# A diffusion trunk on eight cores: the context block projected before its shift is known, loads in order of need, output stores without waits

## Chip, cores, metric

One Trainium2 chip, eight cores (two dies of four). Every core runs the same program on its own share. The metric is device time in microseconds (us) of the slowest core. Some executions fall into a slower state, in which the cores of one die show a lower granted clock; those runs are marked slow and left out of every comparison and every median below (among them one execution each of e1, e6, e10 and e12, two of e2, and some of the kernel before). Ratios below are the mean time of one kernel's fast runs over that of the other's fast runs of the same rounds, so not quite the ratio of the medians that are quoted.

## The reference, cut to what matters

Two layers; each is a mixer and a SwiGLU feed-forward, each sub-layer normalised, modulated by conditioning and added through a gate. One core holds 512 context tokens (**block 0**) and 1024 latent tokens (**blocks 1 and 2**), of 1024 channels.

```python
def ada_terms(cond, w, b):          # six (Bc, 1, D) arrays: shift/scale/gate for mixer and ffn
    mod = (jax.nn.silu(cond) @ w + b)[:, None, :]
    return jnp.split(mod, 6, axis=-1)
# mixer of layer 0:  h = rms_norm(x, g) * (1 + scale) + shift
#   z = h @ w_in                    # pooling input, query, key/value latent, rotary key
#   pooling mixer on z[:512]; multi-head latent attention on the rest
#   context attends to itself; latent attends to 512 cached tokens and its own 1024
# layer 1 mixer: chunked spatial-gating MLP (gMLP). After each mixer: SwiGLU feed-forward.
```

The context's compressed keys and rotary keys of layer 0 are outputs too (`state_ckv`, `state_krope`).

## The kernel before

A Python class writes the instruction streams of the engines. Each piece of work is a generator that yields a unit (`U`) when it needs an engine, a buffer or a PSUM bank. A list scheduler picks the next unit by estimated times; among these is a model of how transfers of the two issuing queues share the DMA engines. So **the order of instructions on each engine follows from the model's constants**, and for some copies and squares the engine too. A different estimate gives a different order in all that follows.

```python
    DMA_RATE = 335.0
    def dma(self, q, out, in_, key, after=None):
        ...
        if last is not None and last != nm and self.known[q].get(k, 0) < self.dtot[k]:
            eng.wait_ge(self.sem[k], self.dtot[k])      # same semaphore, other tile: wait for all before
        ...
        self.queues[q].append([self.t[q] + 300.0, n * esize(in_.dtype) / self.DMA_RATE, ev])
    def _flow(self):                                    # the model of two queues that share the engines
        ...
            if on_a and on_b:
                d = min(ra, rb) * 2
                ra -= d / 2
                rb -= d / 2
    ...
        def load_w0():                                  # weights of the first projections
            yield U("dma")
            P.dma("pool", cb[:], cb_d, "cb")
            yield U("dma", cond=lambda: 7 in ada_ring or st["ada"] >= 8)   # after eight conditioning pieces
            W["ina"] = Multi(P, "w_ina", 8, 672, BF16, 3)
            ... # w_ina (3 loads), w_ukv, cached latent, then the cached rope key krr[3], w_uq, rope tables, w_inu, pool_w
        def k_rope(kb):
            yield U("dve", cond=has("kv%d" % kb), room=(1024, 1024))
            kr = krr[kb]
            sqk = P.alloc("sqkr", [32, 512], BF16)
            kg = P.alloc("kg", [32, 512], BF16)
            P.square(sqk[:], kr[:], engs=("dve", "act"))                   # reads the loaded key
    ...
            # last group of the last feed-forward, block b, row tile m
            resid(ps, l, 5, m, b)
            if store and lastg:
                P.dma("sp", y_out[b, m], x[b][:, m, :], "yout")
    ...
            (0, load_x("xi", (0, 1, 2), {1: landed("d_ada5"), 2: landed("d_wina2")})),   # when x of blocks 1, 2 may start
```

Of the kernel before, what the change touches and what calls it, by code (L numbers as in the profile page):

```python
# [22 lines left out]
def esize(dt):  # L23
    return 2 if dt == BF16 else 4
# [54 lines left out]
class Prog:  # L79


    DMA_RATE = 335.0
# [314 lines left out]
    def dma(self, q, out, in_, key, after=None):  # L397
# [10 lines left out]
        if last is not None and last != nm and self.known[q].get(k, 0) < self.dtot[k]:  # L408
            eng.wait_ge(self.sem[k], self.dtot[k])
            self.known[q][k] = self.dtot[k]  # L410
            evs = evs + [(k, self.dtot[k])]
# [10 lines left out]
        self.queues[q].append([self.t[q] + 300.0, n * esize(in_.dtype) / self.DMA_RATE, ev])  # L422
# [10 lines left out]
    def _flow(self):  # L433

        ia, ib = 0, 0
        A, B = self.queues["sp"], self.queues["pool"]
        t, ra, rb = 0.0, (A[0][1] if A else 0.0), (B[0][1] if B else 0.0)
        while ia < len(A) or ib < len(B):
# [4 lines left out]
            if on_a and on_b:  # L443
                d = min(ra, rb) * 2
                ra -= d / 2
                rb -= d / 2
# [180 lines left out]
def build():  # L627
# [32 lines left out]
    with ExitStack() as es:  # L660
# [16 lines left out]
        P.memset("dve", ones[:], 1.0)  # L677
        EPSI = {1024: 0, 384: 1, 256: 2, 96: 3}
# [20 lines left out]
        ada_ring = {}  # L699
        hid = [{}, {}]  # L700
# [5 lines left out]
        def ada_dma():  # L706
            for k in range(48):
                yield U("dma", room=(lambda: [4096] + keep(0)) if k >= 20 else 4096, cond=lambda k=k: k < 8 or (k < st["ada"] + 3 and (k < 20 or "ffn0" in flags) and "win_loaded" in flags))
                ada_ring[k] = P.alloc("adaw", [128, 8, 256], BF16)
                P.dma("pool", ada_ring[k][:], ada_d[k], "ada%d" % (k % 8))  # L710
# [3 lines left out]
        def ada():  # L714
            for k in range(48):
# [4 lines left out]
                l, c0 = divmod(2 * k, 48)  # L720
# [8 lines left out]
                for (l_, w, n) in ((0, 0, 8), (0, 1, 20), (1, 0, 32), (1, 1, 44)):  # L729
# [21 lines left out]
        def xnorm(l, w, b, cond, done, last=False):  # L751
            need = {(0, 0): 8, (0, 1): 20, (1, 0): 32, (1, 1): 44}[(l, w)]
# [29 lines left out]
            for kc in range(8):  # L782
                if last:
                    yield U(("dve", "act"), reads=[xb[:, kc, :]])
                    P.affine(hb[:, kc, :], xb[:, kc, :], AA[:, l, w, kc, ci:ci + 1], mscal(l, sh, kc, b))
# [5 lines left out]
                P.back(tmp)  # L791
            if last:
# [4 lines left out]
            flags.add(done)  # L797

# [13 lines left out]
        def load_w0():  # L812
            yield U("dma")
            P.dma("pool", cb[:], cb_d, "cb")
            yield U("dma", cond=lambda: 7 in ada_ring or st["ada"] >= 8)
# [3 lines left out]
            flags.add("ina_loaded")  # L819
            W["ukv"] = P.alloc("w_ukv", [128, 2, 1024], BF16)  # L820
            P.dma("pool", W["ukv"][:], wukv_d, "wukv")
            ckvn[3] = P.alloc("ckvn", [128, 2, 512], BF16)
            P.dma("pool", ckvn[3][:], cckv, "cckv")
            krr[3] = P.alloc("krr", [32, 512], F32)
            P.dma("sp", krr[3][:], ckr, "ckr")
            flags.add("kv3")
            W["uq"] = P.alloc("w_uq", [128, 3, 768], BF16)
            P.dma("pool", W["uq"][:], wuq_d, "wuq")
# [4 lines left out]
            W["inu"] = Multi(P, "w_inu", 8, 512, BF16, 4)  # L833
            for q in range(2):
                P.dma("pool", W["inu"].tiles[q][:], wiu_d[:, 4 * q:4 * q + 4, :], "winu%d" % q)
            W["pw"] = P.alloc("pw", [128, 4, 128], BF16)
            P.dma("pool", W["pw"][:], pw_d, "pw")
            flags.add("win_loaded")

        rope, ckvn, cqn, krr, uT = {}, {}, {}, {}, {}  # L840

        def win_norm(b, j0, nj, dst, g0, nn, copy=None):
# [3 lines left out]
            for j in range(nj):  # L846
# [4 lines left out]
                ps = pss[j]  # L851
                P.mmg(ps[:], [(wa[:, kc, (j0 + j) * 128:(j0 + j + 1) * 128], hb[:, kc, :]) for kc in range(8)])
                sq = P.tmp(BF16)
                P.square(sq[:], ps[:])
                sqs.append(sq)
# [15 lines left out]
        def win_q(b):  # L871
# [4 lines left out]
            drop("h%d" % b, 3, h[b])  # L876
            drop("ina", 6, W["ina"])

        def win_kv(b):
# [5 lines left out]
            yield U("pe", reads=[hb[:], wa[:]], bank=1)  # L885
            ps = P.bank()
            P.mmg(ps[0:32, :], [(wa[:, kc, 640:672], hb[:, kc, :]) for kc in range(8)])
# [736 lines left out]
```

## Time and profile before

| | before |
|---|---|
| time, fast runs | 1264.77 to 1265.47 us |
| profiled run, span of the slowest core (core 0) | 1268.0 us |
| TensorE busy, share of the span | 90% |
| first projection matmul, median of 8 cores | 68.2 us |
| long attention (blocks 1 and 2), first and last score matmul, median | 192.4 and 350.4 us |
| first matmul of the first feed-forward, median | 389.3 us |
| end of TensorE's last matmul, median | 1245.0 us |

The milestones come from TensorE's instructions on all eight cores. They say where the time lies better than shares do: the head (to 68), the mixer of layer 0 (to 389), the dense rest, and a tail in which only stores run. The lines are shown in the prediction.

### The profile page before, as it was taken

How to read it: one execution, taken by the hardware profiler on the slowest of the kernel's cores; microseconds unless marked ns; L12 is line 12 of the kernel's file. 1: busy time of each engine (PE TensorE's matmuls, PEld its weight loads, DVE VectorE, ACT ScalarE, POOL GpSimd, SP SyncE). 2: the span in 40 equal slices, each digit the busy share in tenths (PEclk: the TensorE clock that was granted, in tenths of full speed). 3: DMA queues.
4: the chain of work that ended last, by engine and by line, in shares of the span. 5: the costliest groups of instructions: out<-in, count | busy, mean ns of one | idle time of the engine just before them, and what ended most of it. 6: DMA issues, size and time to landing. Idle time of an engine off the chain costs nothing.

```text
span 1268.0 us, 15934 instructions; the slowest of 8 cores (1254.1 to 1268.0 us)
## 1 busy us (share of the span) xinstructions
PE 1135.3 (90%) x5849; PEld 509.5 (40%) x5849; DVE 575.4 (45%) x960; ACT 383.3 (30%) x611; POOL 186.4 (15%) x286
## 2 busy tenths in 40 slices
PE   2178976998889999999999998999899999999995
PEld 1033433333234545444444433444444444444442
DVE  0068767645137312241342587675542134134264
ACT  2146665768943111101101063343321110110100
POOL 5334223330020120100100000220401010000000
PEclk9998986999999999999999998999899999999998
DMA  9970263360079999630555010000826062030004
GB/s 176 208 165 26 38 110 70 62 205 1 1 109 169 169 171 165 103 64 1 91 97 104 2 34 1 1 1 1 139 45 116 1 112 38 1 67 1 1 17 183
DMA packets 31001, 97.03 MB, mean 77 GB/s; under 512 B 4288, under 2 KB 5856, under 8 KB 30928
## 3 DMA queue, kind: packets, MB, share of 16 engines
q0 software_dynamic: 21424, 73.58, 34.8%
q1 hardware_dynamic: 9504, 22.44, 5.7%
q8 instruction: 50, 0.82, 0.3%
q14 instruction: 23, 0.19, 0.1%
HBM read 159.19 MB, written 6.88 MB: 131 GB/s over the span
## 4 chain that ended last, share of the span: by engine, by line
PE 75%; DVE 9%; DMA 7%; ACT 4%; issue 2%; POOL 0%; SPq 0%; ACTq 0%; DVEq 0%; POOLq 0%
PE pp L492 75%; DMA adaw_106<-ada_w 2%; DMA krr_131<-ckr 2%; DMA adaw_4159<-ada_w 2%; ACT pt_1380 L511 1%; ACT pt_1379 L511 1%; ACT pt_1381 L511 1%; DMA qT_627<-tb_68 1%; DMA qT_1382<-tb_70 1%; ACT pt_1378 L511 1%; DVE tf_81 L526 0%; DVE tf_82 L526 0%; DVE tf_79 L526 0%; DVE tf_77 L526 0%; SPq L413 0%
## 5 line engine op out<-in xcount | busy, mean ns | idle before, releaser
L511 ACT ACTIVATE tf_79<-pp 128x512 f32<-128x512 f32 x22 | 13.1, 597 | 185.4 <-PE pp L492 185.4
L511 ACT ACTIVATE tf_80<-pp 128x512 f32<-128x512 f32 x23 | 13.7, 597 | 65.7 <-PE pp L492 65.7
L511 ACT ACTIVATE tf_77<-pp 128x512 f32<-128x512 f32 x23 | 13.7, 597 | 65.2 <-PE pp L492 65.1
L511 ACT ACTIVATE tf_82<-pp 128x512 f32<-128x512 f32 x22 | 13.1, 597 | 62.7 <-PE pp L492 62.7
L511 ACT ACTIVATE tf_78<-pp 128x512 f32<-128x512 f32 x22 | 13.1, 597 | 62.5 <-PE pp L492 62.5
L511 ACT ACTIVATE tf_81<-pp 128x512 f32<-128x512 f32 x20 | 11.9, 597 | 60.4 <-PE pp L492 60.4
L515 DVE TENSOR_TENSOR sqkr_160<-krr_131 32x512 bf16<-32x512 f32 x1 | 0.7, 678 | 54.3 <-DMA krr_131<-ckr 54.3
L526 DVE SCALAR_TENSOR_TENSOR x_2288<-pp,mod_47,x_2288 128x512 f32<-128x512 f32 x20 | 15.0, 751 | 14.3 <-PE pp L492 13.8
L526 DVE SCALAR_TENSOR_TENSOR x_2285<-pp,mod_47,x_2285 128x512 f32<-128x512 f32 x20 | 15.0, 751 | 14.3 <-PE pp L492 13.8
L526 DVE SCALAR_TENSOR_TENSOR x_2286<-pp,mod_47,x_2286 128x512 f32<-128x512 f32 x20 | 15.0, 751 | 14.2 <-PE pp L492 13.7
L526 DVE SCALAR_TENSOR_TENSOR x_2287<-pp,mod_47,x_2287 128x512 f32<-128x512 f32 x20 | 15.0, 750 | 13.7 <-PE pp L492 13.3
L526 DVE SCALAR_TENSOR_TENSOR x_2413<-pp,mod_47,x_2413 128x512 f32<-128x512 f32 x20 | 15.0, 750 | 12.3 <-PE pp L492 12.0
L526 DVE SCALAR_TENSOR_TENSOR x_2429<-pp,mod_47,x_2429 128x512 f32<-128x512 f32 x20 | 14.9, 751 | 11.6 <-PE pp L492 11.3
L526 DVE SCALAR_TENSOR_TENSOR x_2414<-pp,mod_47,x_2414 128x512 f32<-128x512 f32 x20 | 14.9, 750 | 10.7 <-PE pp L492 10.4
L526 DVE SCALAR_TENSOR_TENSOR x_2416<-pp,mod_47,x_2416 128x512 f32<-128x512 f32 x20 | 14.9, 750 | 10.7 <-PE pp L492 10.4
L526 DVE SCALAR_TENSOR_TENSOR x_2415<-pp,mod_47,x_2415 128x512 f32<-128x512 f32 x20 | 14.9, 750 | 10.6 <-PE pp L492 10.4
L526 DVE SCALAR_TENSOR_TENSOR x_2431<-pp,mod_47,x_2431 128x512 f32<-128x512 f32 x20 | 14.9, 750 | 8.7 <-PE pp L492 8.5
L526 DVE SCALAR_TENSOR_TENSOR x_2430<-pp,mod_47,x_2430 128x512 f32<-128x512 f32 x20 | 14.9, 749 | 8.7 <-PE pp L492 8.5
L526 DVE SCALAR_TENSOR_TENSOR x_2432<-pp,mod_47,x_2432 128x512 f32<-128x512 f32 x20 | 14.9, 750 | 8.7 <-PE pp L492 8.5
L511 ACT ACT_TABLE_LOAD x11 | 14.1, 1283 | 12.0 <-DVE tf_81 L526 6.6
L492 PE MATMUL pp<-scT_51,adaw_96 128*128 128x2 bf16 x16 | 0.6, 165 | 14.6 <-DMA adaw_96<-ada_w 14.6
L492 PE MATMUL pp<-tb_71,ones_46 128*128 128x512 bf16 x7 | 2.9, 408 | 11.6 <-ACT tb_71 L511 11.6
(2007 smaller groups left out, 2875.7 us busy)
## 6 DMA issues: line engine op xcount, KB each, us to landing
w_uq_133<-w_uq POOLq DMA_DIRECT2D x1, 576.0 KB, 60.5
x_87<-x_in SPq DMA_DIRECT2D x1, 512.0 KB, 4.8
x_88<-x_in SPq DMA_DIRECT2D x1, 512.0 KB, 8.7
adaw_96<-ada_w POOLq DMA_DIRECT2D x1, 512.0 KB, 12.2
x_89<-x_in SPq DMA_DIRECT2D x1, 512.0 KB, 13.7
adaw_98<-ada_w POOLq DMA_DIRECT2D x1, 512.0 KB, 17.0
x_90<-x_in SPq DMA_DIRECT2D x1, 512.0 KB, 18.4
adaw_100<-ada_w POOLq DMA_DIRECT2D x1, 512.0 KB, 20.1
```

What stands on the lines that cost most here:

```text
L492: ins = self.op("pe", lambda g: g.matmul(out, lhsT, rhs, start=start, stop=stop, **kw), [lhsT, rhs], [out], (c, 190), inc=inc)
L511: return self.op("act", lambda g: g.activation(out=out, in_=in_, func=func, bias=bias, scale=scale, **kw), reads, writes, d)
L515: return self.op(e, lambda g: g.tensor_tensor(out=out, in0=in0, in1=in1, op=op), [in0, in1], [out], self._d(e, out, [in0, in1], "tt"))
L526: return self.op(e, lambda g: g.scalar_tensor_tensor(out=out, in0=in0, scalar=sc, in1=in1, op0=op0, op1=op1), reads, [out], self._d(e, out ...
```

## The change

Three intents, and new constants for the scheduler's model of transfers. (1) `h = n*s + t` with `n` the normalised x, `s` the scale, `t` the shift; so `w.h = w.(n*s) + w.t`. For the context block the four conditioning pieces of the scale load first, `n*s` is projected, and `w.t`, a row of 672 numbers, is added by a matmul with one row. The pooling projection of that block uses a second, full copy of h. (2) Loads come in the order in which they are needed. (3) The output stores no longer wait for the pair before. Also, the VectorE work on the rope key is queued only when the key has landed. Cut to its core:

```diff
-    DMA_RATE = 335.0
+    DMA_RATE = 325.0
-    def dma(self, q, out, in_, key, after=None):
+    def dma(self, q, out, in_, key, after=None, final=False):
-        if last is not None and last != nm and self.known[q].get(k, 0) < self.dtot[k]:
+        if last is not None and last != nm and not final and self.known[q].get(k, 0) < self.dtot[k]:
+        first = 4000.0 if q == "pool" and not self.queues[q] else 0.0
-        self.queues[q].append([self.t[q] + 300.0, n * esize(in_.dtype) / self.DMA_RATE, ev])
+        self.queues[q].append([self.t[q] + 300.0 + first, n * esize(in_.dtype) / self.DMA_RATE, ev])
-                d = min(ra, rb) * 2              # _flow: equal shares
+                d = min(ra * 3.0, rb * 1.5)      # _flow: one third and two thirds
...
+        ORD = [4, 5, 6, 7, 0, 1, 2, 3] + list(range(8, 48))      # scale pieces first
...
+            early = last and b == 0              # xnorm: context block, scale alone, later a second copy
+                    P.affine(hu[:, kc, :], xb[:, kc, :], AA[:, l, w, kc, ci:ci + 1], mscal(l, sh, kc, b))
...
+        def bias0():                             # the row: shift times w_ina
+                P.mmg(ps[0:1, 0:c1 - c0], [(sh[:, kc:kc + 1], wa[:, kc, c0:c1]) for kc in range(8)])
...
+        def shift0(ps, j0, n):
+            P.mm(ps[0:n, :], brow[0][:, j0:j0 + n], ones_row[:], start=False, stop=True)
...          load_w0: w_ina after four pieces; w_ukv, w_uq, w_inu, cached latent, pool_w after eight;
             rope key and rope tables only after all x
+            yield U("dve", reads=[kr[:]], room=(1024, 1024))      # k_rope: do not queue before the key is there
+            yield U("dve", reads=[kg[:]], room=4096)              # k_proj likewise
-            P.dma("sp", y_out[b, m], x[b][:, m, :], "yout")
+            P.dma("sp", y_out[b, m], x[b][:, m, :], "yout", final=True)
-            (0, load_x("xi", (0, 1, 2), {1: landed("d_ada5"), 2: landed("d_wina2")})),
+            (0, load_x("xi", (0, 1, 2), {1: landed("d_ada6"), 2: landed("d_wuq")})),
+            (2.5, bias0()),
```

(The two state outputs, of 512 and 64 KB, also get a semaphore each.)

More of the change, by code (lines that the diff above doesn't have):

```diff
@@ L443, in _flow @@
             if on_a and on_b:
-                d = min(ra, rb) * 2
-                ra -= d / 2
-                rb -= d / 2
+                d = min(ra * 3.0, rb * 1.5)
+                ra -= d / 3.0
+                rb -= d / 1.5
             elif on_a:
@@ L677, in build @@
         P.memset("dve", ones[:], 1.0)
+        ones_row = P.alloc("ones_row", [1, 512], BF16)
+        P.memset("dve", ones_row[:], 1.0)
         EPSI = {1024: 0, 384: 1, 256: 2, 96: 3}
@@ L707, in ada_dma @@
             for k in range(48):
-                yield U("dma", room=(lambda: [4096] + keep(0)) if k >= 20 else 4096, cond=lambda k=k: k < 8 or (k < st["ada"] + 3 and (k < 20 or "ffn0" in flags) and "win_loaded" in flags))
+                yield U("dma", room=(lambda: [4096] + keep(0)) if k >= 20 else 4096,
+                        cond=lambda k=k: k < 4 or (k < 8 and "ina_loaded" in flags) or (k < st["ada"] + 3 and (k < 20 or "ffn0" in flags) and "win_loaded" in flags))
                 ada_ring[k] = P.alloc("adaw", [128, 8, 256], BF16)
-                P.dma("pool", ada_ring[k][:], ada_d[k], "ada%d" % (k % 8))
+                P.dma("pool", ada_ring[k][:], ada_d[ORD[k]], "ada%d" % (k % 8))
         st = {"ada": 0}
@@ L719, in ada @@
                 yield U("pe", reads=[sl[:]], bank=1, rank=rank)
-                l, c0 = divmod(2 * k, 48)
+                l, c0 = divmod(2 * ORD[k], 48)
                 ps = P.bank()
@@ L728, in ada @@
                 st["ada"] = k + 1
-                for (l_, w, n) in ((0, 0, 8), (0, 1, 20), (1, 0, 32), (1, 1, 44)):
+                for (l_, w, n) in ((0, 0, 4), (0, 1, 20), (1, 0, 32), (1, 1, 44)):
                     if k + 1 == n:
@@ L751, in xnorm @@
         def xnorm(l, w, b, cond, done, last=False):
-            need = {(0, 0): 8, (0, 1): 20, (1, 0): 32, (1, 1): 44}[(l, w)]
+            early = last and b == 0
+            need = 4 if early else {(0, 0): 8, (0, 1): 20, (1, 0): 32, (1, 1): 44}[(l, w)]
             sh = 0 if w == 0 else 3
@@ L784, in xnorm @@
                     yield U(("dve", "act"), reads=[xb[:, kc, :]])
-                    P.affine(hb[:, kc, :], xb[:, kc, :], AA[:, l, w, kc, ci:ci + 1], mscal(l, sh, kc, b))
+                    P.affine(hb[:, kc, :], xb[:, kc, :], AA[:, l, w, kc, ci:ci + 1], 0.0 if early else mscal(l, sh, kc, b))
                     continue
@@ L791, in xnorm @@
                 P.back(tmp)
+            if early:
+                flags.add(done)
+                yield U(("dve", "act"), cond=lambda: st["ada"] >= 8, room=(4096, 4096))
+                hu = Multi(P, "h", 8, 512, BF16, 4)
+                for kc in range(8):
+                    yield U(("dve", "act", "pool"), reads=[xb[:, kc, :]])
+                    P.affine(hu[:, kc, :], xb[:, kc, :], AA[:, l, w, kc, ci:ci + 1], mscal(l, sh, kc, b))
+                h["u"] = hu
+                flags.add("hu")
             if last:
@@ L797, in xnorm @@
             flags.add(done)
+        brow = {}
+        def bias0():
+            yield U("pe", cond=lambda: st["ada"] >= 8 and "ina_loaded" in flags, bank=1, room=(1344, 32))
+            sh = P.alloc("sh0", [128, 8], BF16)
+            P.ts("dve", sh[:], mod[:, 0, 0:8, 0], 1.0, None, ALU.mult)
+            row = brow[0] = P.alloc("brow", [1, 672], BF16)
+            wa = W["ina"]
+            for c0, c1 in ((0, 512), (512, 672)):
+                yield U("pe", reads=[sh[:], wa[:]], bank=1)
+                ps = P.bank()
+                P.mmg(ps[0:1, 0:c1 - c0], [(sh[:, kc:kc + 1], wa[:, kc, c0:c1]) for kc in range(8)])
+                P.copy(row[:, c0:c1], ps[0:1, 0:c1 - c0])
+            P.free(sh)
+            flags.add("brow")
         def resid(ps, l, term, m, b):
@@ L812, in load_w0 @@
         def load_w0():
-            yield U("dma")
-            P.dma("pool", cb[:], cb_d, "cb")
-            yield U("dma", cond=lambda: 7 in ada_ring or st["ada"] >= 8)
+            yield U("dma", cond=lambda: 3 in ada_ring)
             W["ina"] = Multi(P, "w_ina", 8, 672, BF16, 3)
@@ L819, in load_w0 @@
             flags.add("ina_loaded")
+            yield U("dma", cond=lambda: 7 in ada_ring)
+            P.dma("pool", cb[:], cb_d, "cb")
             W["ukv"] = P.alloc("w_ukv", [128, 2, 1024], BF16)
             P.dma("pool", W["ukv"][:], wukv_d, "wukv")
+            W["uq"] = P.alloc("w_uq", [128, 3, 768], BF16)
+            P.dma("pool", W["uq"][:], wuq_d, "wuq")
+            W["inu"] = Multi(P, "w_inu", 8, 512, BF16, 4)
+            for q in range(2):
+                P.dma("pool", W["inu"].tiles[q][:], wiu_d[:, 4 * q:4 * q + 4, :], "winu%d" % q)
             ckvn[3] = P.alloc("ckvn", [128, 2, 512], BF16)
             P.dma("pool", ckvn[3][:], cckv, "cckv")
+            W["pw"] = P.alloc("pw", [128, 4, 128], BF16)
+            P.dma("pool", W["pw"][:], pw_d, "pw")
+            yield U("dma", cond=has("xi1"))
             krr[3] = P.alloc("krr", [32, 512], F32)
@@ L826, in load_w0 @@
             flags.add("kv3")
-            W["uq"] = P.alloc("w_uq", [128, 3, 768], BF16)
-            P.dma("pool", W["uq"][:], wuq_d, "wuq")
             rope["C"] = P.alloc("ropeC", [128, 1024], F32)
@@ L832, in load_w0, with project @@
             P.dma("sp", rope["S"][:], rope_d[1], "ropeS")
-            W["inu"] = Multi(P, "w_inu", 8, 512, BF16, 4)
-            for q in range(2):
-                P.dma("pool", W["inu"].tiles[q][:], wiu_d[:, 4 * q:4 * q + 4, :], "winu%d" % q)
-            W["pw"] = P.alloc("pw", [128, 4, 128], BF16)
-            P.dma("pool", W["pw"][:], pw_d, "pw")
             flags.add("win_loaded")
         rope, ckvn, cqn, krr, uT = {}, {}, {}, {}, {}
+        def project(b, ps, j0, n):
+            hb, wa = h[b], W["ina"]
+            pairs = [(wa[:, kc, j0:j0 + n], hb[:, kc, :]) for kc in range(8)]
+            for kc, (l_, r_) in enumerate(pairs):
+                P.mm(ps[0:n, :], l_, r_, start=(kc == 0), stop=(kc == 7 and b != 0), inc=(kc == 7))
+        def shift0(ps, j0, n):
+            P.mm(ps[0:n, :], brow[0][:, j0:j0 + n], ones_row[:], start=False, stop=True)
         def win_norm(b, j0, nj, dst, g0, nn, copy=None):
@@ L850, in win_norm @@
                     pss = [P.bank(hold=True) for _ in range(nj)]
-                ps = pss[j]
-                P.mmg(ps[:], [(wa[:, kc, (j0 + j) * 128:(j0 + j + 1) * 128], hb[:, kc, :]) for kc in range(8)])
-                sq = P.tmp(BF16)
-                P.square(sq[:], ps[:])
-                sqs.append(sq)
+                project(b, pss[j], (j0 + j) * 128, 128)
+                if b != 0:
+                    sqs.append(P.tmp(BF16))
+                    P.square(sqs[j][:], pss[j][:])
+            if b == 0:
+                for j in range(nj):
+                    yield U("pe", cond=has("brow"), tb=1)
+                    shift0(pss[j], (j0 + j) * 128, 128)
+                    sqs.append(P.tmp(BF16))
+                    P.square(sqs[j][:], pss[j][:])
             for j in range(nj):
@@ L875, in win_q @@
             flags.add("q%d" % b)
-            drop("h%d" % b, 3, h[b])
+            drop("h%d" % b, 3 if b else 2, h[b])
             drop("ina", 6, W["ina"])
@@ L884, in win_kv @@
             cf = P.alloc("ckvf", [128, 2, 512], F32) if b == 0 else None
-            yield U("pe", reads=[hb[:], wa[:]], bank=1)
+            yield U("pe", reads=[hb[:], wa[:]], bank=1, cond=has("brow") if b == 0 else None)
             ps = P.bank()
-            P.mmg(ps[0:32, :], [(wa[:, kc, 640:672], hb[:, kc, :]) for kc in range(8)])
+            project(b, ps, 640, 32)
+            if b == 0:
+                shift0(ps, 640, 32)
             P.copy(krr[b][:], ps[0:32, :])
             if b == 0:
-                P.dma("sp", skr_out, krr[b][:], "stout")
+                P.dma("sp", skr_out, krr[b][:], "skr")
             yield from win_norm(b, 3, 2, ckvn[b], 3, 256, cf)
             if b == 0:
-                P.dma("sp", sckv_out, cf[:], "stout")
+                P.dma("sp", sckv_out, cf[:], "sckv")
                 P.free(cf)
             flags.add("kv%d" % b)
-            drop("h%d" % b, 3, hb)
+            drop("h%d" % b, 3 if b else 2, hb)
             drop("ina", 6, wa)
         def win_u(b):
-            yield U("pe", cond=has("h0_%d" % b, "win_loaded"))
+            yield U("pe", cond=has("h0_%d" % b if b else "hu", "win_loaded"))
             part = "ctx" if b == 0 else "lat"
             n = 544 if b == 0 else 1040
-            hb, wu = h[b], W["inu"]
+            hb, wu = h[b or "u"], W["inu"]
             for m in range(4):
@@ L920, in win_u @@
             flags.add("u%d" % b)
-            drop("h%d" % b, 3, hb)
+            if b:
+                drop("h%d" % b, 3, hb)
+            else:
+                P.free(hb)
             drop("inu", 3, wu)
@@ L999, in k_proj @@
             yield U("pe", cond=has("kv%d" % kb, "kr%d" % kb), room=4096)
+            sqk, kg = krot[kb]
+            yield U("dve", reads=[kg[:]], room=4096)
             kt = kT[(kb, hg)] = P.alloc("kT", [96, 4, 512], BF16)
-            sqk, kg = krot[kb]
             P.copy(kt[64:96, :, :], bass.AP(kg.t, 0, [[512, 32], [0, 4], [1, 512]]), engs=("dve",))
@@ L1492, in build @@
         P.run(streams)
-        for k in ("d_yout", "d_stout"):
+        for k in ("d_yout", "d_skr", "d_sckv"):
             nc.sync.wait_ge(P.sem[k], P.dtot[k])
```

## The prediction

> **What bounds the kernel now.** I read the page first (engine shares and the 40 slices), then the busy time by stretch, then TensorE's instructions, the waits and the DMA landings of the first 110 us, then the last 30 us. The stretches, with columns start:end, length, busy us (x instructions) of PE, PEld, DVE, ACT, POOL, then granted clock, DMA share, GB/s:
>
> ```profile
> 0.00:34.00 34.00, 7.27 (x104) 3.84 (x104) 2.61 (x14) 8.17 (x12) 18.95 (x30) 1.00 0.96 176
> 34.00:70.00 36.00, 5.66 (x42) 2.03 (x43) 8.58 (x19) 5.33 (x9) 12.03 (x13) 1.00 1.04 212
> 70.00:86.00 16.00, 15.91 (x63) 6.01 (x62) 10.71 (x19) 6.16 (x11) 2.99 (x3) 1.00 0.98 214
> 86.00:196.00 110.00, 92.03 (x562) 42.32 (x560) 82.82 (x139) 67.52 (x138) 36.63 (x70) 0.87 0.30 58
> 196.00:361.00 165.00, 138.88 (x610) 53.72 (x610) 79.47 (x105) 125.95 (x138) 35.39 (x49) 0.93 0.27 64
> 361.00:475.00 114.00, 112.22 (x779) 54.49 (x780) 47.76 (x93) 25.28 (x40) 17.53 (x32) 0.99 1.04 167
> 475.00:1252.00 777.00, 762.48 (x3693) 346.87 (x3691) 341.96 (x573) 144.88 (x266) 62.88 (x91) 0.99 0.29 53
> 1252.00:1268.00 16.00, 0.84 (x4) 0.20 (x2) 1.50 (x2) 0.00 (x0) 0.00 (x0) 0.61 0.53 195
> ```
>
> The reader is to see two places where TensorE has nothing to do: the first 70 us (57 us idle) with the DMA engines full, and the last 16 us with the DMA half full. From 361 to 1252 TensorE is 98% busy; nothing in the change makes that work shorter, it can only begin earlier. In between (86 to 361) no engine is full: chains across engines and the exponentials set the pace.
>
> Why the head lasts 70 us, from TensorE's instructions and the waits:
>
> ```profile
> 33.05 0.56 PE L492 MATMUL pp<-scT_51,adaw_106 128*128 128x2 bf16 x16 [2.89 <-DMA adaw_106<-ada_w]
> ...
> 63.58 0.56 PE L492 MATMUL pp<-scT_51,adaw_117 128*128 128x2 bf16 x16 [2.17 <-DVE mod_47 L515]
> 64.01 0.56 PE L492 MATMUL pp<-scT_51,adaw_119 128*128 128x2 bf16 x16
> 69.56 1.44 PE L492 MATMUL pp<-h_398,w_ina_121 128*128 128x512 bf16 x3 [4.99 <-DVE h_398 L521]
> ```
>
> ```profile
> DVE sqkr_160 L515 <- DMA krr_131<-ckr: 54.3, 1, 54.3
> ```
>
> The eight conditioning pieces had landed by 42.2 us (issue 5.86 plus 36.3 to landing for the eighth), the first projection weights by 55.3. But VectorE's queue stood from 6.6 to 60.8 behind a square of the cached rope key, a 64 KB load queued after two others. All additions into mod and the first h stood behind it. So it is a wait in the wrong place as well as DMA time. The chain that ended last names the same two transfers:
>
> ```profile
> 4.82 28.09 DMA adaw_106<-ada_w
> ...
> 36.08 24.74 DMA krr_131<-ckr
> ```
>
> The tail, from SyncE's queue: the last matmul starts at 1252.24 and the stores leave in pairs every 2.8 us, each pair behind the landing of the one before (eleven waits of 1.2 to 2.0 us):
>
> ```profile
> 1259.70 0.81 SPq L413 DMA_DIRECT2D y<-x_2430  x2
> 1262.47 0.81 SPq L413 DMA_DIRECT2D y<-x_2431  x2
> 1265.23 0.81 SPq L413 DMA_DIRECT2D y<-x_2432  x2
> ```
>
> TensorE makes a pair of output tiles in 1.73 us (eight matmuls of 0.216). Stores lag more with each pair; the last leaves 11.5 us after VectorE finished it (1253.7). The same gap of 15.2 to 15.5 us between TensorE's end and the span's end stands on cores 0, 1, 2, 3 and 5.
>
> **What the Trainium skill says.** "DMA: Bandwidth & Descriptors", section "Issuing engines are not separate DMA queues": transfers started by SyncE and GpSimd interleave on the same 16 engines. The trace agrees: with GpSimd's queue alone a conditioning piece (1 MB of float32 read) lands about every 3.2 us; with x loading on SyncE's queue it takes 4 to 5.5. So reordering moves landings but cannot shorten the whole load. Same page, "Anatomy of one DMA": most of the fixed cost, about 2 us, is the receipt before the semaphore. Agrees: an output store takes 2.0 to 2.3 us to land, and a wait per pair pays it each time. "TensorE: Matmul & The Clock Gate", "The HAM clock gate": half rate after some 3.4 us of idleness, full rate after as long busy. Agrees: starts of 512-column matmuls are 0.43 us apart at 70 us, 0.216 from 75 us on. So early matmuls that stand among waits cost double.
>
> **The change, part by part.** The order of the changed kernel's instructions was read on each engine.
>
> Loads. GpSimd's queue becomes: the four scale pieces, the projection weights (three), the four shift pieces, then the rest; the rope key goes behind all x blocks. With the paces of before (no small first load; 3.2 us a MB while alone) I get landings: scale pieces 13.7, 19, 22.7, 25.7; weights 29, 32, 34; shift pieces 37, 40.5, 43.8, 47.5. x of block 1 is released by the seventh piece instead of the sixth, at 43.8 instead of 32.9; at the old pace (11.4 us for the first of four, 26.5 for all) it lands at 55 to 70, ten us later than before (59.5). Block 2 follows to about 88 (before 86.0). So the load ends no sooner.
>
> Context block. VectorE no longer stands behind the rope key. Normalised x is there at about 31, scaled h at 34 to 35, weights at 34: the projection starts near 34 instead of 69.6. The three query tiles (24 matmuls of 0.43, then 0.22) run into the 40s, TensorE then waits for the eighth piece (47.5), forms the row (8 matmuls of 512 and 8 of 160 columns, cold: 8 x 0.43 + 8 x 0.135 = 4.5 us), and adds it with six 512-column matmuls. Added matmul work: 8 x 0.216 + 8 x 0.067 + 6 x 0.216 = 3.6 us warm, all before 71 us, in time that was idle. A second scaled and shifted copy of h (eight operations of 0.5 to 0.8 us on VectorE and ScalarE, about 5 us) falls near 48 to 53, idle too. But ScalarE's queue interleaves these squares with squares of block 1, so the chain keeps the pace of x landing at 55 to 70: context queries and keys are done near 71, not near 55.
>
> Position at 71. By then TensorE has done what before was done at about 85: gain 14. Next, the query, pooling and value work of the context block fills 71 to 87, while block 1 is normalised; block 1's projection starts at about 87. Before, a comparable point in TensorE's order (matmul columns at the warm rate, summed: 33.4 us before, 34.4 after) was reached at 109: gain 22.
>
> Start of the long attention. Before, it starts at 195.97, which is 110 us after the last x landed, for 71 us of warm matmul time still to do (1.5 us per us). After, 59 us remain once x has landed at about 88: 59 x 1.53 = 90, so 178: gain 18. The stretch 196 to 361 is led by ScalarE (0.76 busy; 96 exponentials of 1.12 us) and keeps its length but for 2.4 us more of matmul work inside it. Taken: 16 us, of which everything later moves along, since feed-forward loads start when attention's buffers come free.
>
> Output stores. No wait per pair: the last store leaves behind VectorE at about 1253.8, 0.4 to issue, 2.2 to land: 1256.4 in old time instead of 1268.0. A pair now goes out every 1.73 us, 524 KB or 303 GB/s; the bursts of before run at 320 to 380 GB/s in a slice, so the queue should hold this, with perhaps 1 us of lag. Gain 11, given as 9.5 to 11.7.
>
> Sum: 16 + 11 = 27; 1265.3 - 27 = 1238.
>
> **Rivals.** (a) The head is bound by the load alone. Last x lands at 88 against 86, and then comes a fixed chain of normalisation, projection, rope and transposing copies to the attention. For it: between 86 and 196 VectorE was 75% busy and TensorE waited for VectorE again and again. Against it: much of that VectorE and TensorE work belonged to the context block and is now done earlier. If true the head gives 0 to 6 us, total 1248 to 1254. (b) The new order puts x squares ahead of context work in in-order queues and delays x of block 1 by 10 us; if x lands later than my 70 and 88 (it shares the engines with weights ranked earlier), VectorE and ScalarE stand as they once stood for the rope key. Head gain 5 to 10: 1244 to 1250. (c) Stores become bound by the DMA: all eight cores write at once, and at 250 GB/s 6.3 MB takes 25 us instead of TensorE's 20.7: tail gain 7 instead of 11. For it only that no stretch shows a steady write. (d) Better than thought: all of the 22 us position gain reaches the attention and fewer cold matmuls follow; with the stores 33, so 1232.
>
> **Range and chances.** Tail 7 to 12, head 6 to 24 with 16 the middle: sums 16 to 36. Range 1228 to 1249. Faster by 2% means under 1240.0, which needs 25.3 of my 27: little better than even, 0.57. Within 2%: 0.41. Slower by 2%: 0.02, since the two idle places are real and the added work lies in one of them.
>
> **What would show it.** Right: the first projection matmul at 32 to 37; no wait of VectorE of tens of us for the rope key; the row's matmuls near 48 to 53; the long attention's first matmul at 173 to 185; no wait of SyncE on an earlier y store, and a gap of 3.5 to 6 us from TensorE's last matmul to the span's end; a gain that hardly grows between 361 and the last matmul. Wrong: attention starting at 190 or later (rivals a, b; then VectorE or ScalarE show long waits for x between 55 and 90); stores still leaving after 1.73 us pacing with a growing lag (c); a feed-forward stage that waits for its weights and gives the gain back.

## The result

The changed kernel took 1235.64 us (median of four fast runs, 1234.61 to 1236.16), ratio 0.9766, 95% interval 0.9746 to 0.9785: 2.3% faster.

| median of the 8 cores, us | before | after | earlier by |
|---|---|---|---|
| first projection matmul | 68.2 | 36.2 | 32.0 |
| long attention, first score matmul | 192.4 | 168.9 | 23.5 |
| long attention, last score matmul | 350.4 | 339.3 | 11.1 |
| first matmul of the first feed-forward | 389.3 | 378.1 | 11.2 |
| end of TensorE's last matmul | 1245.0 | 1225.8 | 19.2 |
| time (slowest core, median of the fast runs) | 1265.3 | 1235.6 | 29.6 |

Read down the last column: the gain shrinks by 12 us inside the attention, grows by 8 in the dense part and by 10.4 in the tail. The changed kernel's busy time by stretch (core 0; columns as in the prediction: stretch, length, PE, PEld, DVE, ACT, POOL, granted clock, DMA share, GB/s), cut where its own stages begin:

```profile
0.00:34.00 34.00, 5.82 (x72) 3.34 (x72) 11.95 (x28) 6.62 (x9) 15.53 (x26) 1.00 0.95 176
34.00:70.00 36.00, 25.30 (x146) 10.58 (x149) 10.59 (x22) 12.72 (x21) 7.57 (x11) 0.86 1.03 200
70.00:86.00 16.00, 13.21 (x52) 5.11 (x52) 14.97 (x25) 11.29 (x27) 12.61 (x14) 0.89 1.03 240
86.00:171.00 85.00, 71.40 (x418) 32.77 (x425) 66.87 (x114) 46.22 (x93) 31.45 (x50) 0.87 0.31 65
171.00:346.00 175.00, 147.16 (x691) 59.58 (x703) 88.31 (x127) 132.93 (x159) 33.91 (x43) 0.91 0.31 71
346.00:460.00 114.00, 110.30 (x735) 53.36 (x747) 49.04 (x92) 27.38 (x42) 18.52 (x34) 0.99 0.92 151
460.00:1229.00 769.00, 755.47 (x3656) 346.90 (x3727) 344.72 (x578) 137.81 (x258) 64.43 (x93) 1.00 0.31 57
1229.00:1233.00 4.00, 0.97 (x5) 0.24 (x3) 1.72 (x3) 0.00 (x0) 0.00 (x0) 1.00 0.73 269
```

In 34 to 70 TensorE is now busy for 25.3 us instead of 5.7, in part at half rate (clock 0.86), under a DMA that is as full as before. The attention's stretch, 165 us before, is 175 us, and its PE, DVE and ACT work grew with it (ACT 126 to 133, DVE 79 to 88). So attention began earlier with more of its surroundings unfinished. What was unfinished shows by tile: the keys. The lines are those of e1 (the kernel before with other stores, same order) and e13 (the changed kernel again), whose names come without buffer numbers, each from its first to its last score matmul (groups by line: shapes, count; busy, mean ns; idle before):

```profile
L561 ACT CAST kT<-pp 64x512 bf16<-64x512 f32 x4 | 2.3, 580 | 3.2 <-PE pp L492 3.1
L563 ACT CAST kT<-pp 64x512 bf16<-64x512 f32 x16 | 9.3, 579 | 1.6 <-PE pp L494 1.2
```

With four more casts on VectorE, five key tiles (`kT`) were formed inside the attention instead of one, and VectorE's work on them (`tb<-kT`) took 9.0 us there instead of 1.7. The last stretch, 16 us before, is 4.

TensorE's instructions at the head, of the changed kernel:

```profile
36.53 1.06 PE L494 MATMUL pp<-h_277,w_ina_105 128*128 128x512 bf16 x2 [8.33 <-ACT h_277 L513]
...
48.23 1.44 PE L494 MATMUL pp<-w_ina_105,sh_79_426 128*1 128x512 bf16 x3 [1.33 <-DVE sh_79_426 L523]
...
52.80 0.58 PE L494 MATMUL pp<-ones_row_53,brow_428 1*128 1x512 bf16 x1
```

The row is formed from 48.2 to 52.8 us, cold (at half rate), as worked out. VectorE's longest waits of the first 90 us are now for TensorE's conditioning matmuls and for x, not for the rope key (waits of VectorE, 0 to 90 us: total, times, longest):

```profile
DVE mod_47 L517 <- PE pp L494: 10.1, 5, 4.0
DVE tb_76 L517 <- DMA x_118<-x_in: 5.9, 1, 5.9
```

The end, from SyncE's queue and from TensorE:

```profile
1226.60 1.19 SPq L413 DMA_DIRECT2D y<-x_2693  x2
1228.68 0.99 SPq L413 DMA_DIRECT2D y<-x_2694  x2
1230.05 1.21 SPq L413 DMA_DIRECT2D y<-x_2695  x2
```

```profile
1229.38 0.60 PE L494 MATMUL pp<-a_8697,wd_9507 128*128 128x512 bf16 x2
```

The last pair leaves with TensorE's last matmul, in TensorE's pace of about 1.73 us a pair, and the span ends 3.1 us after it (3.1 to 3.9 on the eight cores). From the first of these stores to the end of the span the cores move 276 to 287 GB/s each, with all eight storing at once.

### The profile page after: what moved, and what is told of

Read it like the earlier page. It is cut to its first block, busy times and chain, and to the rows that moved or that the text cites. A ratio compares the mean times of both kernels' runs of the same rounds, so it can differ in the third digit from the quotient of the medians.

```text
span 1233.1 us, 15863 instructions; the slowest of 8 cores (1227.4 to 1233.1 us)
## 1 busy us (share of the span) xinstructions
PE 1129.6 (92%) x5762; PEld 511.9 (42%) x5871; DVE 588.2 (48%) x984; ACT 375.0 (30%) x607; POOL 184.0 (15%) x269
## 4 chain that ended last, share of the span: by engine, by line
PE 73%; DVE 10%; DMA 8%; ACT 5%; issue 2%; POOL 1%; SPq 0%; ACTq 0%; DVEq 0%; POOLq 0%
PE pp L494 73%; DMA adaw_115<-ada_w 3%; DMA x_120<-x_in 2%; DMA wo_2316<-ab_w_out 2%; ACT pt_1134 L513 1%; ACT pt_1136 L513 1%; DMA qT_1263<-tb_68 1%; DVE tf_84 L528 1%; DVE tf_81 L528 0%; DVE tf_80 L528 0%; DVE tf_83 L528 0%; DVE tf_79 L528 0%; DVE tf_82 L528 0%; DVE tb_76 L517 0%; ACT pt_1135 L513 0%
## 5 line engine op out<-in xcount | busy, mean ns | idle before, releaser
L528 DVE SCALAR_TENSOR_TENSOR x_2451<-pp,mod_47,x_2451 128x512 f32<-128x512 f32 x20 | 15.0, 751 | 10.9 <-PE pp L494 10.6
L528 DVE SCALAR_TENSOR_TENSOR x_2452<-pp,mod_47,x_2452 128x512 f32<-128x512 f32 x20 | 14.9, 751 | 10.8 <-PE pp L494 10.6
L528 DVE SCALAR_TENSOR_TENSOR x_2454<-pp,mod_47,x_2454 128x512 f32<-128x512 f32 x20 | 14.9, 751 | 10.7 <-PE pp L494 10.4
L528 DVE SCALAR_TENSOR_TENSOR x_2453<-pp,mod_47,x_2453 128x512 f32<-128x512 f32 x20 | 14.9, 750 | 10.7 <-PE pp L494 10.4
L528 DVE SCALAR_TENSOR_TENSOR x_2694<-pp,mod_47,x_2694 128x512 f32<-128x512 f32 x20 | 14.8, 749 | 8.9 <-PE pp L494 8.9
L494 PE MATMUL pp<-h_277,w_ina_105 128*128 128x512 bf16 (+1 forms) x17 | 5.8, 454 | 8.3 <-ACT h_277 L513 8.3
L513 ACT ACT_TABLE_LOAD x7 | 9.0, 1283 | 10.6 <-DVE tf_82 L528 4.9
L517 DVE TENSOR_TENSOR mod_47<-pp,vecs_43 128x4 f32<-128x4 f32 x48 | 6.7, 154 | 11.3 <-PE pp L494 11.2
## 6 DMA issues: line engine op xcount, KB each, us to landing
x_90<-x_in SPq DMA_DIRECT2D x1, 512.0 KB, 11.6
adaw_99<-ada_w POOLq DMA_DIRECT2D x1, 512.0 KB, 15.5
```

What stands on the lines that cost most here:

```text
L494: ins = self.op("pe", lambda g: g.matmul(out, lhsT, rhs, start=start, stop=stop, **kw), [lhsT, rhs], [out], (c, 190), inc=inc)
L513: return self.op("act", lambda g: g.activation(out=out, in_=in_, func=func, bias=bias, scale=scale, **kw), reads, writes, d)
L517: return self.op(e, lambda g: g.tensor_tensor(out=out, in0=in0, in1=in1, op=op), [in0, in1], [out], self._d(e, out, [in0, in1], "tt"))
L528: return self.op(e, lambda g: g.scalar_tensor_tensor(out=out, in0=in0, scalar=sc, in1=in1, op0=op0, op1=op1), reads, [out], self._d(e, out ...
```

## The experiments

Milestones below are medians of the eight cores in each run's profile. "Before" lay at 1266.9, 1266.5 and 1263.6 us in the three calls (e1 to e4; e5 to e9; e10 to e13; no e8), so ratios to it are safer than microseconds across calls.

A caution for all that follows. Compared instruction by instruction in the traces (core 1), e1, e2, e6 and e7 keep the order of every engine, but for what they add. The edits of e4, e5, e9, e10 and e11 also made the scheduler choose another order: some 600 to 900 of TensorE's 5849 to 5871 matmuls stand elsewhere, against 600 in e3, which changes only the order and the engine of some pieces. So a difference in these five is the worth of an edit together with the order that it brought; none of them holds the order still.

### The stores alone, and all but the stores

`e1_stores_only` is the kernel before with one edit, `e2_no_stores` the changed kernel without it:

```diff
-    P.dma("sp", y_out[b, m], x[b][:, m, :], "yout")
+    P.dma("sp", y_out[b, m], x[b][:, m, :], "yout", final=True)     # e1; e2 is the reverse in the changed kernel
```

> The kernel before, with nothing changed but the output stores, which no longer wait for the pair before; the order of all other instructions is the same. My theory (the stores' waits were the whole of the tail): about 11 to 12 us faster, 1253 to 1254, with the gap from TensorE's last matmul to the span's end down from 15.3 to 3 to 4 us. Rival (stores become bound by the DMA): 7 us or less, with a gap of 8 us. If the stores' gain in the changed kernel came partly from the earlier stages, this run shows less than 11.

> The changed kernel with the stores' waits put back; all other instructions in the changed order. If the two parts simply add, 11 to 12 us slower than the changed kernel, 1247 to 1248, and 17 to 18 us faster than the kernel before. If they help or hinder each other, the two single gains do not sum to the 29.7 us of the whole.

e1: 1255.7 us, ratio 0.991 (0.9892 to 0.9928), 11.2 us between the medians. From TensorE's end to the span's end 3.1 us on every core. All else stayed (attention's end 351.8, before 350.4). The stores' step is shown.

e2: two of its four runs were slow; the two fast ones took 1250.7 and 1251.6, 15.5 us more than the changed kernel (about 14 by the ratios to before), not 11 to 12. It is 15.7 us faster than the kernel before, so the two single gains, 11.2 and 15.7, sum to 27 of the 29.6. The gap after TensorE's end was 17.6 to 18.8 us against 14.8 to 15.7 in the kernel before: a pair of stores took about 3.2 us here (24 stores in 35.7 us) instead of 2.85. Why a pair took longer is not settled; with two fast runs on another chip I would not build on the 15.5. TensorE's end, 1228.4, was 1.4 to 2.6 us later than in the changed kernel's two profiles (1227.0 and 1225.8).

### The row trick taken away

`e5_no_row` keeps the changed loads, gates, model and stores, but projects the context block once scale and shift are both there:

```diff
-            early = last and b == 0
+            early = False
-            (2.5, bias0()),
# and: no shift0, no second copy hu, stop flag on the eighth projection matmul for all blocks
```

> The changed kernel with its load order, but the context block is projected only once scale and shift are both there, as before; no row of the shift, no second copy of h. My step in the prediction: with the trick the projection starts at 34 but the chain then keeps the pace of x of block 1 (landing 55 to 70), so the trick's own worth is small: the first projection matmul at 48 to 50 here, the long attention's end within 2 us of the changed kernel's 339, the whole 0 to 4 us slower than the changed kernel (1236 to 1240). Rival: the trick carries the head's gain, and without it the whole is 8 to 12 us slower (1244 to 1248). The late stages tell a second thing: if the waits of the gMLP's output stage stay away here as well, the trick is not what moved them.

Its first lines of TensorE at the head (core 0):

```profile
47.88 0.57 PE L494 MATMUL pp<-scT,adaw 128*128 128x2 bf16 x16 [2.31 <-DMA adaw<-ada_w]
48.31 6.96 PE L494 MATMUL pp<-h,w_ina 128*128 128x512 bf16 x24
```

The first projection came 12 us later than in the changed kernel, and the attention's last score matmul at 338.8 against 339.3. The time was 1232.8 us, ratio 0.9729 (0.9709 to 0.9748). I had expected 0 to 4 us slower; it was faster. So both were run again:

> The kernel of e5_no_row once more, beside the changed kernel on the same chip and in the same call, since the two differed by only 3 us in different calls. If the row and the second copy cost more than they give, this is 2 to 4 us faster than the changed kernel again; if the difference was the chip's or the call's, within 1 us.

> The changed kernel itself, as the partner of e12_no_row_again in the same call: 1234.5 to 1236.5 if calls agree (the kernel before gave 1265.4 and 1267 in other calls, so up to 1238).

Without the row 1230.4 us, ratio 0.9729 (0.9715 to 0.9744); the changed kernel 1234.6, ratio 0.9763 (0.9749 to 0.9777). **The row and the second copy, with the order that they bring, cost about 4 us.** The attention's end lies at 335.6 without and 340.3 with it. Where the row loses can be summed from the two traces (medians of the cores, from the start to the end of the mixer's output projection): with the row TensorE is idle for 80 us instead of 89, but busy for 295 instead of 282. Of these 13 us, 3.6 are the added matmuls; by my estimate (busy time less columns, at 0.216 us per 512) the other 9 or so are the same matmuls at half rate. The mean granted clock says the same: 0.968 to 0.975 with the row, 0.981 to 0.984 without. So the earlier start filled idle time with slower work. In its attention this version forms no key at all. This version beats both kernels, and it is the simpler one.

### The other parts of the head, one at a time

`e4_rope_key`: the kernel before with the two extra yields of `k_rope` and `k_proj` alone. `e3_model_only`: the kernel before with the new constants of the scheduler's transfer model alone.

```diff
+            yield U("dve", reads=[kr[:]], room=(1024, 1024))          # e4, in k_rope; and likewise in k_proj
-    DMA_RATE = 335.0                                                   # e3
+    DMA_RATE = 325.0                                                   # e3; also the first transfer and the sharing
```

> The kernel before with only the square and the cast of the cached rope key moved later in VectorE's queue, so that it no longer stands behind that load; load order, projection and stores as before. If half the head's gain came from this wait alone, the first projection matmul comes at 50 to 57 us instead of 69.6, the long attention's first matmul at 180 to 188 instead of 192 to 196, and the whole is 5 to 10 us faster. If only the new load order matters (weights come at 55 in the old order, and x of block 1 bounds what follows), the first projection moves but the attention does not: 0 to 3 us.

> The kernel before with only the scheduler's model of transfers changed (rate, first transfer, sharing of two queues), which changes no work but the order in which the scheduler places instructions. It tests where the extra gain between 378 us and the end came from (about 8 us that I had not predicted). Theory M (the new model orders the later stages better): 4 to 8 us faster than before, with the first matmul of the first feed-forward stage where it was (389 us) and the end earlier. Theory L (the later gain comes from weights that start to load earlier, so from the head): no change, within 2 us of 1265.

e4: 1264.4 us, ratio 0.9977 (0.9961 to 0.9993). The 54.3 us wait is gone, and VectorE waits for x in its place:

```profile
DVE tb L515 <- DMA x<-x_in: 31.5, 9, 7.5
...
DVE sqkr L515 <- DMA krr<-ckr: 1.0, 1, 1.0
```

The first projection comes at 60.0 (before 68.2), the attention's end at 350.6 (before 350.4): with VectorE's longest wait of the head gone, and the order that this brought, the whole gained 2.5 us. Its attention even began later, at 201.1, and still ended where it had. That already shows that the first score matmul is a poor mark.

e3: 1277.7 us, ratio 1.008 (1.0064 to 1.0096): the same work in another order (with some copies and squares on another engine) is **10.8 us slower**. Both theories (4 to 8 faster, or no change) fell. The loss lies before the attention's end (363.8, 13 us later); from the first feed-forward to TensorE's end it is 4 us shorter than before.

So is it the loads? `e10_old_model` is e5_no_row with the old constants:

> The kernel of e5_no_row (changed loads, no row, no second copy) with the scheduler's model of transfers as it was before. Put beside e3_model_only (the new model alone made the kernel before 10.8 us slower), it tells whether the new model or the new loads brought the head's gain. If the loads alone bring it: within 3 us of e5_no_row, 1230 to 1236, the long attention ending at 336 to 342 and the late stages again without their waits. If the new model is needed with the new loads: 1240 or more. A third view, that any change of order throws the stretch from 90 to 390 us by several us in either direction, also fits a result outside 1230 to 1236, on the fast side too.

It took 1250.0 us, ratio 0.9884 (0.9869 to 0.9899), with the attention's end at 354.4: 4 us *later* than in the kernel before, though its first projection came at 47.1. Beside e12_no_row_again, the model's constants are worth some 20 us *for* the new loads; beside the kernel before they are worth 11 us *against* the old ones. The parts do not add. All that the constants do is choose the order of instructions, and the engine of some.

### An earlier landing for x

`e9_x_earlier` tests the gate that the prediction named, the landing of x of block 1:

```diff
-            (0, load_x("xi", (0, 1, 2), {1: landed("d_ada6"), 2: landed("d_wuq")})),
+            (0, load_x("xi", (0, 1, 2), {1: landed("d_wina2"), 2: landed("d_wuq")})),
```

> The changed kernel, with the x of block 1 released when the projection weights have landed (34 us) instead of the seventh conditioning piece (43). It should land at 46 to 62 instead of 55 to 69, and the shift pieces some 4 us later. If the landing of x of block 1 gates the head, as I said in the prediction (the chain keeps the pace of x), the long attention's end comes 4 to 8 us earlier and the whole is as much faster (1228 to 1232). If the sum of the load and the work behind it sets the time, nothing moves: within 2 us of 1235.6; if the later shift pieces matter, it is slower.

On core 0 the chain of waits names a quarter of it that went out at 35.8 us and landed at 53.5; in the changed kernel the four landed between 54.9 and 68.5. The time was 1249.0 us, ratio 0.9868 (0.9839 to 0.9898), and the attention ended at 354.8, 15 us later than in the changed kernel. So an earlier x did not bring an earlier mixer; my rule missed even the sign. The run is no clean test of the gate, though. The edit had a price, which the third case of my expectation named: the eighth conditioning piece landed at 51.7 instead of 46.1, two of VectorE's squares of x stood in its queue before the last additions into mod, and the row was formed from 56.2 us instead of 48.2. The order changed too. I can name one new wait, for the small state output, whose buffer is used again:

```profile
DVE pbf L528 <- DMA skr<-krr: 4.6, 1, 4.6
```

It took 25 us to land behind the loads on its queue. That is a part only of the 15; how the rest divides between the late row and the order is not shown.

### What sets the length of the attention

Two runs add about 14 us of work that touches nothing else, to one engine each:

```diff
# e6_more_scalar: after every fourth exponential of the long attention
+    nc.scalar.activation(out=ones_row[64:128, :], in_=ones_row[64:128, :], func=AF.Exp, bias=0.0, scale=0.0)
# e7_more_tensor: in every third step both score matmuls are issued twice
+    P.mm(S[j][:], kt_, qs[j], twice=i % 3 == 1)
```

> The changed kernel, with 24 exponentials of 64 x 512 elements on ScalarE between those of the long attention, written to a spare tile that nobody reads; nothing else moves in any engine's order. About 0.6 us each, 14 us of ScalarE's time in all. Theory S (ScalarE's work sets the length of the long attention): 11 to 14 us slower than the changed kernel, all of it before the attention's end. Theory T (TensorE's work does): 0 to 4 us slower. Theory C (a chain through several engines, each waiting for another): 5 to 10.

> The changed kernel, with 64 of the 192 score matmuls (512 columns, 0.216 us at the full rate) of the long attention issued twice, so 13.8 us more of TensorE's time in the same stretch; the result is unchanged, nothing else moves. Theory S (ScalarE sets the length): 0 to 4 us slower than the changed kernel, or even a gain where the clock stays up. Theory T: 12 to 15 us slower. Theory C: 5 to 10.

ScalarE's lines of e6 (line, operation, tiles, shape, count; busy, mean ns; idle before):

```profile
L513 ACT ACTIVATE pt<-pp,ksc 128x1024 bf16<-128x1024 f32 x96 | 102.6, 1110 | 21.5 <-PE pp L494 21.3
L1270 ACT ACTIVATE ones_row<-ones_row 64x512 bf16<-64x512 bf16 x24 | 15.0, 627 | 0.6
```

The 15.0 us on ScalarE moved the attention's end by 10.6 us (349.9 against 339.3; 9.6 against the changed kernel's other profile), the time to 1244.7 us, ratio 0.9823. The 13.8 us on TensorE moved the end by 12.8 (11.8), the time to 1246.3, ratio 0.9836. By the ratios to before, against the changed kernel's 0.9763 to 0.9766, the costs are 7 and 9 us. e7 rules out theory S (0 to 4 expected), e6 rules out theory T (0 to 4 expected), and C stands: neither engine has slack for 14 us, although ScalarE was 76% and TensorE 84% busy. Both stand in one chain of score matmul, exponential and value matmul.

`e11_deeper` loosens that chain in the e5_no_row version:

```diff
-            DEPTH = 1 if two else 2
+            DEPTH = 2
```

> The kernel of e5_no_row with the long attention's score tiles formed two steps ahead of the value matmuls instead of one. The two runs that added 14 us to ScalarE or to TensorE each lost about 10, so both stand in one chain: score matmul, exponential, value matmul. If the coupling of one step makes it a chain, two steps loosen it: the long attention 5 to 15 us shorter, 1218 to 1228 in all. If PSUM (four pairs of banks, one or two held for the sums) or the other work of TensorE in that stretch sets the pace, nothing: within 3 us of 1233. If the pairs run short, slower, 1236 to 1245.

It took 1239.2 us, ratio 0.9797, 9 us slower than its partner e12_no_row_again. The stretches of e11 (attention, then what was left over, then the output projection):

```profile
190.00:298.00 108.00, 96.92 (x395) 33.11 (x393) 27.16 (x33) 104.13 (x107) 4.83 (x10) 0.99 0.03 7
298.00:331.00 33.00, 16.41 (x76) 6.86 (x76) 28.44 (x30) 13.57 (x25) 15.90 (x17) 0.72 0.65 147
331.00:384.00 53.00, 49.37 (x209) 21.15 (x208) 33.16 (x53) 14.60 (x23) 7.01 (x12) 0.89 1.00 195
```

and those of e12_no_row_again:

```profile
189.00:336.00 147.00, 123.89 (x536) 47.69 (x535) 71.51 (x86) 116.99 (x128) 24.71 (x31) 0.99 0.27 64
336.00:371.00 35.00, 31.80 (x140) 13.73 (x138) 21.08 (x31) 11.73 (x18) 8.44 (x15) 0.95 0.99 155
```

The chain was loosened: the attention took 108 us instead of 147, with ScalarE 96% busy. But VectorE's work (44 us of it) was pushed behind it, where TensorE has little to do: 33 us with TensorE half idle and cold (0.72), then an output projection that takes 53 us instead of 35. A stage that looks 39 us shorter made the whole longer.

## Why the prediction was right or wrong

The time was right (1238 against 1235.6, inside the range), and so was "faster". Step by step, core 0 where the prediction used core 0:

| step | predicted | measured |
|---|---|---|
| first projection matmul | 32 to 37 | 36.5 |
| matmuls of the row | 48 to 53 | 48.2 to 52.8 |
| x of block 1 lands; last x | 55 to 70; 88 | 54.9 to 68.5; 86.3 |
| block 1's projection | 87 | 86.7 |
| attention's first score matmul | 178 (173 to 185) | 171.3 |
| length of the attention | unchanged but for 2.4 | 159.0 before, 172.0 after |
| head's gain at the attention's end | 16 | 11.7 (11.1 median) |
| gain between there and TensorE's end | hardly any | 8.1 (median) |
| gain from the stores | 9.5 to 11.7 | 11.2 alone (e1) |
| sum | 27 | 29.6 |

Two slips of the prediction's own: head 6 to 24 and tail 7 to 12 sum to 13 to 36, not 16 to 36, so its range should have ended at 1252; and the gap that it reads as 15.2 to 15.5 us on five cores is 14.8 to 15.3 there (14.8 to 15.7 on all eight).

**Right and shown.** The landings, the row's place, and the stores (e1). Rival (c) fell: no lag grows, the last pair leaves at TensorE's end. Rival (a) fell: with the last x at the same time (86), the attention ended 11 us earlier.

**Wrong: "position at 71", taken to the attention's first matmul, which then carries the gain.** The prediction said that the attention "keeps its length but for 2.4 us". It grew by 13 on core 0, where five key tiles had to be formed inside it instead of one. The first score matmul marks when one chain is ready, not how much of all engines' work is done: ScalarE and VectorE had 133 and 88 us left at that point against 126 and 79 before. e4 shows the same from the other side (first score matmul 9 us later, last one where it was), and e6 and e7 show that work left on either engine lengthens the stretch. What would have been right was already in the text: the gain of 14 at 71 us, less the 2.4 of added matmuls, is 11.6, and 11.1 was measured. That agreement is one number and may be luck.

**Wrong: "led by ScalarE".** Its 0.76 share did not make it the only pace-maker: 13.8 us of matmuls (e7) cost as much as 15.0 us of exponentials (e6).

**Wrong in attribution: what the head's gain is made of.** I had given it to the early projection, the freed VectorE queue and the loads together, and worked each as if it moved the rest along. Alone, each with the order that it brought, the early projection costs about 4 us (e5, e12, e13), the freed queue brings 2.5 (e4), the model costs 11 (e3), the loads and the freed queue with the old model bring the attention's end 4 us later (e10). Only new loads and new model together bring 12 to 15 us at the attention's end. My figure for the head was near because the sum was near, not because the mechanism was. Rival (b), gating by x of block 1, is not supported either, but not refuted: earlier x came with a later row and made it slower (e9).

**Wrong: "nothing in the change makes that work shorter".** From the first feed-forward's first matmul to TensorE's end the kernel before takes 855.7 us, the changed one 847.7. Part of it can be seen. In the kernel before, TensorE waits at the end of the gMLP twice for VectorE on core 0, and the clock drops (TensorE's instructions; the number in brackets is the wait):

```profile
896.30 1.02 PE L492 MATMUL pp<-h_7141,wg_7727 128*128 128x512 bf16 x4 [2.24 <-DVE tf_78 L526]
897.16 1.85 PE L492 MATMUL pp<-h_7142,wg_7727 128*128 128x512 bf16 x4
899.90 1.87 PE L492 MATMUL pp<-h_7141,wu_7731 128*128 128x512 bf16 x4 [0.89 <-DVE tf_80 L526]
901.56 1.91 PE L492 MATMUL pp<-h_7142,wu_7731 128*128 128x512 bf16 x4
...
904.52 1.03 PE L492 MATMUL pp<-h_7142,wg_7727 128*128 128x512 bf16 x4
```

Four matmuls of 512 columns take 0.86 us at the full rate and about 1.7 here. From the first matmul with the gMLP's spatial weights to TensorE's last matmul, TensorE is idle for 6.4 us before and 1.5 after (medians of the cores). It stays at 5.5 to 6.3 in e1, e3 and e4, which have the old loads, and is 1.0 to 1.9 in e2, e5, e9 and e10, which have the new ones. So this part came with the new loads (the freed queue alone, e4, did not bring it), not with the row and not with the constants, again through the order of instructions; which line of that order I did not isolate. Another 2 us lie in the stage of the first feed-forward (362.7 to 360.7 us), and those appear in e3 too (360.6).

**Open.** Why one order of the same work is 11 to 20 us better than another. From 90 us to the last matmul of the mixer's output projection core 0 took 301 us before, 306 in e3, 289 after and 281 in e12, with TensorE busy 242 to 257 us by the profile. These stretches do not hold quite the same work (213 and 217 us at the full rate before and in e3, 206 and 209 after and in e12, medians by columns), so some 4 to 11 us of it had been done before 90. The rest lies in waits and in half-rate time; no single wait that I found explains it.

## What to carry to other kernels

Judge an early gain at a point where all engines have finished the same work, not at the first instruction of the next stage. A long wait in a trace is worth what follows from removing it in a run, here 2.5 us for 54. And where a list scheduler orders the work, test each part of a change against a changed order with no change of work: here (e3) that alone moved the time by 0.8%, a third of the whole gain, which is more than the loss (0.3%) that the headline part of the change brought.

## What the Trainium skill lacked or had wrong

- "TensorE: Matmul & The Clock Gate", section on the HAM clock gate, gives half rate after at least one idle window of about 3.4 us. In the kernel before it came after a wait of only 2.24 us (the lines at 896 us above): 512-column matmuls ran at 0.43 us from about 897 to 904, and the slow matmuls cost some 3 us beyond the waits (four groups, about 0.8 us each for three of them and 0.4 for one). Another section of that page, "A second HAM failure mode: psum-queue depth-cycling", says that frequent short idle times make the clock oscillate too, but no section says how busy a window must be to keep the full rate.
- "DMA: Bandwidth & Descriptors", "Anatomy of one DMA", gives a fixed cost of about 2 us and a term for size, for transfers that GpSimd issues. The output stores at the end, which SyncE issues, agree (2.1 to 2.6 us to landing for 256 KB, median by kernel). It has no figure for a small transfer behind others on its queue: the 64 KB state output took 28.1 us to land in the changed kernel, 6.7 in the kernel before, and in e9 VectorE waited 4.6 us for it.
- No page that I read says that the order of the same instructions on in-order engines can be worth as much as an optimisation: 10.8 us (e3) against the kernel before, some 20 us (e10 against e12_no_row_again).
